# Weight splits in halves on VectorE, gate values and queries scaled on ScalarE, modulation tiles across four column groups

## The chip, the cores and the metric

One core of one Trainium2 chip runs the whole program: two layers of a transformer that denoises 512 latent tokens beside 256 context tokens. The metric is device time in microseconds, from launch to end; lower is better. Engines: PE is TensorE (matmuls), DVE VectorE, ACT ScalarE, POOL GpSimd, SP the queue that issues most DMAs.

## The reference

```python
for l in range(2):
    mod_l = silu(c) @ ada_w[l] + ada_b[l]        # shifts, scales and gates of latents
    mod_c = silu(c_ctx) @ ada_w[l] + ada_b[l]    # and of context
    hl, hc = modulate(xl, ...), modulate(xc, ...)
    yl, yc = even_mixer(...) if l == 0 else odd_mixer(...)
    xl = xl + g1 * yl
    xl = xl + g2 * conv_ffn(modulate(xl, ...))   # the same for xc in layer 0

def even_mixer(...):
    p = h @ w_in                                 # for hl and hc
    y1 = hgrn2_mixer(...)                        # gated linear attention, 4 heads, 2 directions
    u, v = gelu(p_u), rms_norm(gelu(p_v)) * vnorm_w
    y2 = u * (ws @ v + bs)                       # spatial gate, 4 groups of 128 columns
    return concat(y1, y2) @ w_out

def odd_mixer(...):
    y1 = fourier_mix(...)
    q, k, v = mla_project(...)                   # low-rank, rms_norm per head, 64 rotary columns
    return concat(y1, attend(q, k, v)) @ w_out
```

All of it is float32 with a tight tolerance.

## The kernel before, in words

**Precision.** A float32 matmul is made of three (`mm3`, L508 to L510): each operand is split into a rounded part (h, `wh`) and a remainder (l, `wl`), and h·h, h·l and l·h are summed. So each chunk of weights, 128x1024 mostly, is loaded (`raw`, SP's queue, L329), copied and rounded by ScalarE (L486), and its remainder is a subtraction: on GpSimd in one piece for the kinds in `on_pool` (L498), in two GpSimd halves for `by_half` (L495), in one half on GpSimd and one on VectorE for `down1` (L490), and on VectorE in one piece for the rest.

**Order of chunks.** `_Stream` holds the chunks in a fixed order: 4 `ev_v`, 16 `ev_in` (four a head), 8 `ev_vp`, 4 more `ev_in` (20 to 23, one a gate group), 16 `ev_out` (two passes of eight), then the feed-forward network, and layer 1. `next()` hands out one chunk and prepares the following one, at most one ahead for most kinds.

**Order of instructions.** The prologue (up to about 70 us) has its order on PE, ACT and DVE written out by hand. All else goes through a planner that orders each engine's queue by its own costs and the order of the program; `tc.high_priority(200)` lets an instruction ahead. Side work lies in generators: `tick()`, called between matmul groups, moves the generator "gla" (linear attention of one head) one step, and "ada" (modulations) at every second call; `drain()` runs one to its end.

**Mixer of layer 0.** Per head, `proj` (L795) computes four projections, while `gla` (L806) works on the head before: seven levels, at each of which PE multiplies blocks (L827, or L855 at the last two) and VectorE multiplies queries (L868) and keys (L870) by decay factors, 128x768. After the levels come states and outputs (L918, L923: squares summed on ScalarE), an inverse square root of small VectorE operations (`rsqrt`, L460 to L465), the scaling L930, a `yield`, transposes (L939) and the gating L940. Then the gate values: 8 `ev_vp` chunks, gelu and square sums (L988 to L992), `rsqrt`, six GpSimd operations that scale the values (L997), and `drain("gla")`, which ends head 3. Then, for each of four groups: projection `ev_in` 20+g, gelu (L1005), the spatial matmul (L1011), L1014 and L1018 on VectorE, and the split of the product (L1020 on ScalarE, L1021 on GpSimd).

**Output projection.** Two passes of eight chunks, the first on half of the tokens, with residuals (L1028), the norm's squares (L612, L613) and, in the second pass, the modulation of the first pass's tokens (L647 to L649) on VectorE; the up-projection follows.

**Modulations.** `ada_group` computes 16 blocks of 128 values as a product of the two condition vectors (a 32-column stationary operand) with tiles of 512 KB, (k, hf): k is the block of the contraction, hf the half of the 2048 columns. PE's array is used in four groups of 32 columns, `ps[32 * q:...]`, and a matmul streams 512 columns of the tile:

```python
for j in range(2):
    q = 2 * hf + j
    T.matmul(ps[32 * q:32 * q + 32, :], sc_pad[:, k, :], t[:, j * 512:(j + 1) * 512],
             start=(k == 0), stop=(k == KD - 1))
```

Then a copy (L585), four transposes (L589) and four additions of the bias (L594) put the values feature-major into `mods`. In layer 1 the tiles go into buffers named kt, and the generator is moved one tile at a time.

**Layer 1.** `l0.close()` (L1334) frees layer 0's buffers. Then come the token projections `od_f`, `od_kv`, `od_q`. After `lx.close()` (L1429) the embedding norms `pewb` are loaded (L1433) and the rotary table (L1435); VectorE scales the keys' rotary columns into kp0 (six operations, L1464), GpSimd copies (L1466, L1471), VectorE rotates (L1364 to L1369) and scales the table by pewb (L1470). Then, per pair of heads, keys (L1611 to L1614), values (`project_v`), queries, their statistics, and `scale_queries` (one VectorE operation L1571 and two GpSimd operations L1574), transposes and scores.

Of the kernel before, what the change touches and what calls it, by code (L numbers as in the profile page):

```python
# [415 lines left out]
def backbone(ctx: ExitStack, tc, w, xt, ada, vec, cst, msk, rop, wst, bs, pew, out):  # L416
# [68 lines left out]
    def split(kind, raw, h, l):  # L485
        S.copy(h, raw)  # L486
        if kind[:5] == "down1":
            n = raw.shape[-1] // 2
            for e, c in ((G, slice(0, n)), (V, slice(n, 2 * n))):
                e.tensor_tensor(l[:, c], raw[:, c], h[:, c].bitcast(F32), op=ALU.subtract)  # L490
            return
        if kind in by_half:
            for c in range(2):
                c = slice(c * raw.shape[-1] // 2, (c + 1) * raw.shape[-1] // 2)
                G.tensor_tensor(l[:, c], raw[:, c], h[:, c].bitcast(F32), op=ALU.subtract)  # L495
            return
        e = G if kind in on_pool else V
        e.tensor_tensor(l, raw, h.bitcast(F32), op=ALU.subtract)  # L498
# [68 lines left out]
    def ada_group(l, g, rest, by=1):  # L567
        base = (l * 3 + g) * 16
        ps = bank("ad")
        for k in range(KD):  # L570
            for hf in range(2):
                i = base + 2 * k + hf
                ada_load(i + 1)
                t = ada_raw.pop(i)
                for j in range(2):
                    q = 2 * hf + j
                    T.matmul(ps[32 * q:32 * q + 32, :], sc_pad[:, k, :], t[:, j * 512:(j + 1) * 512],  # L577
                             start=(k == 0), stop=(k == KD - 1))
            if k % by < by - 1:
# [8 lines left out]
        for b in range(4):  # L588
            T.transpose(pt[:, b * P:(b + 1) * P], asb[:, b * P:(b + 1) * P], ident)  # L589
        o = mods[l][:, g * 16:(g + 1) * 16, :].rearrange("p (j b) c -> p b j c", b=4)  # L590
        i0 = pt[:].rearrange("p (b j r) -> p b j r", b=4, r=32)[:, :, :, 0:2]
        i1 = vcol("ada_b", l * 48 + g * 16, 16).rearrange("p (j b) -> p b j", b=4).unsqueeze(3)
        for b in range(4):
            V.tensor_tensor(o[:, b], i0[:, b], i1[:, b].to_broadcast([P, 4, 2]), op=ALU.add)  # L594
        yield
# [210 lines left out]
    def gla(h, QG, FF, Y):  # L806
# [34 lines left out]
        for lv in range(7):  # L841
# [25 lines left out]
            qa = pick(QQ, 0, dd)  # L867
            V.tensor_tensor(qa, qa, pick(FF[:], NT + m, [[2 * m, nb], [-(NT + m), 2], [0, m]]), op=ALU.mult)  # L868
            ka = pick(KK, 0, dd)
            V.tensor_tensor(ka, ka, pick(FF[:], m, [[2 * m, nb], [NT - m, 2], [0, m]]), op=ALU.mult)  # L870
            ta = pick(FF[:], 0, [[NT, 2], [2 * m, nb]])
# [56 lines left out]
        for s, (a0, n) in enumerate(SEGS):  # L928
# [65 lines left out]
    rsqrt(ms[:], mr[:], 24)  # L994
    for c in range(6):
        a = vp[c // 3][:, c % 3, :].rearrange("p (g d) -> p g d", g=4)
        G.tensor_tensor(a, a, mr[:, c * 4:c * 4 + 4].unsqueeze(2).to_broadcast([P, 4, P]), op=ALU.mult)  # L997
    drain("gla")
    for g in range(4):
        ps = proj(("ev_in", 20 + g), X)  # L1000
        U = xcp.tile([P, 2, NT], F32, tag="xc", name="U")
        Y[4 + g] = xslot()
# [428 lines left out]
    l1c = ctx.enter_context(tc.tile_pool(name="l1c", bufs=1, side="right"))  # L1431
    pewb = l1c.tile([P, 128], F32, name="pewb")
    nc.scalar.dma_start(pewb[:], pew.to_broadcast([P, 128]))  # L1433
    rope_t = l1c.tile([P, 512], F32, name="rope_t")
# [25 lines left out]
    kpe = kt()  # L1460
    kp0 = tp.tile([P, 6, 64], F32, tag="t2k", name="kp0")
    kp2 = lt(F32)[:].rearrange("p a b -> p (a b)")[:, 0:768].rearrange("p (c g d) -> p c g d", c=6, g=2)
    for c in range(6):
        V.scalar_tensor_tensor(kp0[:, c, :], kvr[c][:, 256:320], kr[:, 6 + c:7 + c], pewb[:, 64:128],  # L1464
                               op0=ALU.mult, op1=ALU.mult)
    G.tensor_copy(kp2[:, 0:2, 0, :], kp0[:, 0:2, :])  # L1466
    rope(kp2[:, 2:6, 0, :], kp0[:, 2:6, :])

    t8 = rope_t[:].rearrange("p (n d) -> p n d", d=64)
    V.tensor_tensor(t8, t8, pewb[:, 0:64].unsqueeze(1).to_broadcast([P, 8, 64]), op=ALU.mult)  # L1470
    G.tensor_copy(kp2[:, :, 1, :], kp2[:, :, 0, :])  # L1471

# [95 lines left out]
    def scale_queries(p, rq, rp, s24):  # L1568
        r = r28[p % 2][:, 0:16].rearrange("p (a b) -> p a b", b=4)
        pe = rp.rearrange("p (j g d) -> p j g d", j=4, g=2)  # L1570
        V.tensor_tensor(pe, pe, r[:, :, 2:4].unsqueeze(3).to_broadcast([P, 4, 2, 64]), op=ALU.mult)  # L1571
        q4 = rq.rearrange("p j (g d) -> p j g d", g=2)
        for j in (slice(0, 2), slice(2, 4)):
            G.tensor_tensor(q4[:, j], q4[:, j], r[:, j, 0:2].unsqueeze(3).to_broadcast([P, 2, 2, P]), op=ALU.mult)  # L1574

# [304 lines left out]
```

## Time and profile before

| | us |
|---|---|
| median of 3 runs (lowest, highest) | 1649.61 (1648.12, 1650.98) |
| the profiled execution | 1649.35 |
| its span | 1647.6 |
| PE busy | 1591.9 (97%) |
| VectorE busy | 1140.8 (69%) |
| ScalarE busy | 703.4 (43%) |
| GpSimd busy | 649.1 (39%) |

The span runs from the first to the last instruction that the profiler saw on the core; the execution adds 1.75 us around it. The mean granted clock of TensorE is 0.992 of full speed. Busy time of one engine overlaps that of the others; idle time in brackets behind a row is that of the row's engine just before it.

### The profile page before, as it was taken

To read this page: it belongs to the slowest core of one execution; us is meant where nothing else is said; L and a number is where in the kernel's file an instruction comes from. 1 tells how busy PE (TensorE), PEld (TensorE's weight loads), DVE (VectorE), ACT (ScalarE), POOL (GpSimd) and SP (SyncE) were. 2 spreads that over 40 slices of the span, in tenths; PEclk is the share of its full clock that TensorE was granted. 3 is DMA by queue.
4 is the path that set the end of the run, shared out by engine and by line. 5 is a ranking of instruction groups with operands and counts; after the bars stand their busy time and mean duration, and the time that the engine had idled before them with its cause. 6 is when DMAs were issued, how large, how long until landed. Compare 5 with 4: busy or idle time off the path is not lost.

```text
span 1647.6 us, 28314 instructions
## 1 busy us (share of the span) xinstructions
PE 1591.9 (97%) x11206; PEld 1420.5 (86%) x11206; DVE 1140.8 (69%) x2134; ACT 703.4 (43%) x1328; POOL 649.1 (39%) x421
## 2 busy tenths in 40 slices
PE   8999999989999999999999999898899899999998
PEld 7777777678989999999999989676799898999997
DVE  5447675753565666676666775767874799999984
ACT  4323333523444333233332444465665555555551
POOL 1221223344625566565665513331208322323321
PEclk9999999999999999999999999999999999999999
DMA  9453434333412121222212322752105223223222
GB/s 355 159 187 116 142 116 137 120 102 103 130 50 64 61 80 55 74 77 62 80 55 75 90 68 82 250 171 93 52 27 167 90 85 108 103 90 116 103 78 77
DMA packets 53205, 175.11 MB, mean 106 GB/s; under 512 B 5712, under 2 KB 7760, under 8 KB 53072
## 3 DMA queue, kind: packets, MB, share of 16 engines
q1 hardware_dynamic: 51632, 170.66, 31.1%
q10 hardware_dynamic: 1440, 2.64, 0.4%
q8 instruction: 88, 1.44, 0.3%
q14 instruction: 45, 0.37, 0.1%
HBM read 171.18 MB, written 2.10 MB: 105 GB/s over the span
## 4 chain that ended last, share of the span: by engine, by line
PE 79%; DVE 14%; ACT 2%; DMA 2%; issue 2%; POOL 1%; DVEq 0%; SPq 0%; ACTq 0%; POOLq 0%
PE mm L508 17%; PE mm L510 16%; PE mm L509 16%; PE aux L508 7%; PE aux L509 7%; PE aux L510 7%; PE aux L577 2%; DVE qk L870 1%; DVE qk L868 1%; DVE wp L387 1%; PE aux L1143 1%; PE mm L1730 1%; DMA x<-in_xt_dram 1%; DMA raw<-in_w_dram 1%; PE aux L1749 1%
## 5 line engine op out<-in xcount | busy, mean ns | idle before, releaser
L498 POOL TENSOR_TENSOR wl<-raw,wh 128x1024 fp32r<-128x1024 f32 (+5 forms) x100 | 210.2, 2104 | 356.6 <-ACT wh L486 304.5
L486 ACT CAST wh<-raw 128x1024 fp32r<-128x1024 f32 (+5 forms) x155 | 146.5, 947 | 141.0 <-PE mm L509 63.8
L387 POOL TENSOR_TENSOR wp<-sum,wp 128x512 fp32r<-128x512 f32 x80 | 115.9, 1454 | 163.4 <-ACT wp L385 153.9
L508 PE MATMUL mm<-xt,wh 128*128 128x256 f32 (+1 forms) x384 | 135.1, 353 | 0.9 <-ACT xt L648 0.9
L510 PE MATMUL mm<-xt,wl 128*128 128x512 f32 (+1 forms) x384 | 129.4, 338 | 0.0
L509 PE MATMUL mm<-xt,wh 128*128 128x512 f32 (+1 forms) x384 | 129.3, 337 | 0.0
L509 PE MATMUL mm<-slot,wh 128*128 128x512 f32 (+1 forms) x336 | 113.4, 338 | 1.0 <-POOL slot L1253 0.7
L508 PE MATMUL mm<-slot,wh 128*128 128x512 f32 (+1 forms) x336 | 113.5, 339 | 1.0 <-ACT slot L1252 1.0
L510 PE MATMUL mm<-slot,wl 128*128 128x512 f32 (+1 forms) x336 | 113.1, 337 | 0.0
L385 ACT CAST wp<-sum 128x512 fp32r<-128x512 f32 x100 | 60.8, 620 | 122.2 <-PE aux L509 61.5
L1028 DVE SCALAR_TENSOR_TENSOR xl<-mm,mods,xl 128x512 f32<-128x512 f32 (+1 forms) x84 | 58.5, 696 | 70.7 <-PE mm L510 70.2
L495 POOL TENSOR_TENSOR wl<-raw,wh 128x512 fp32r<-128x512 f32 (+2 forms) x50 | 55.7, 1135 | 129.1 <-ACT wh L486 123.6
L387 POOL TENSOR_TENSOR wp<-raw,wp 128x512 fp32r<-128x512 f32 x60 | 80.0, 1341 | 52.3 <-ACT wp L385 52.3
L385 ACT CAST wp<-raw 128x512 fp32r<-128x512 f32 x100 | 62.1, 621 | 78.5 <-DMA raw<-in_w_dram 27.7
L508 PEld LDWEIGHTS mm<-xt,wh 128*128 128x128 f32 x384 | 72.0, 188 | 27.0 <-issue 16.8
L508 PE MATMUL mm<-kt,wp 128*128 128x256 f32 x320 | 90.4, 282 | 3.8 <-ACT t L1216 3.8
L490 POOL TENSOR_TENSOR wl<-raw,wh 128x512 fp32r<-128x512 f32 x22 | 35.7, 1622 | 138.0 <-DVE t L1245 92.3
L510 PE MATMUL mm<-kt,wp 128*128 128x256 f32 x320 | 89.8, 281 | 0.0
L509 PE MATMUL mm<-kt,wp 128*128 128x256 f32 x320 | 89.7, 280 | 0.0
L510 PEld LDWEIGHTS mm<-xt,wl 128*128 128x128 f32 x384 | 72.3, 188 | 8.2
L509 PEld LDWEIGHTS mm<-xt,wh 128*128 128x128 f32 x384 | 72.2, 188 | 8.3
L509 PE MATMUL mm<-lt,wh 128*128 128x256 f32 (+2 forms) x236 | 78.1, 331 | 1.2 <-DVE lt L1253 1.2
(390 smaller groups left out, 5272.7 us busy)
## 6 DMA issues: line engine op xcount, KB each, us to landing
raw<-in_w_dram SPq DMA_DIRECT2D x162, 512.0 KB, 3.5
ada_t<-in_ada_dram SPq DMA_DIRECT2D x80, 512.0 KB, 4.4
raw<-in_w_dram SPq DMA_DIRECT2D x31, 384.0 KB, 3.1
wp<-in_w_dram SPq DMA_DIRECT2D x20, 512.0 KB, 4.4
kt<-in_ada_dram SPq DMA_DIRECT2D x16, 512.0 KB, 7.0
raw<-in_w_dram SPq DMA_DIRECT2D x10, 256.0 KB, 2.6
xl<-in_xt_dram SPq DMA_DIRECT2D x2, 1024.0 KB, 8.0
out_dram<-xl SPq DMA_DIRECT2D x8, 256.0 KB, 2.0
```

The source lines that it names most:

```text
L385: S.copy(h, a)
L387: e.tensor_tensor(l, a, h.bitcast(F32), op=ALU.subtract)
L486: S.copy(h, raw)
L490: e.tensor_tensor(l[:, c], raw[:, c], h[:, c].bitcast(F32), op=ALU.subtract)
L495: G.tensor_tensor(l[:, c], raw[:, c], h[:, c].bitcast(F32), op=ALU.subtract)
L498: e.tensor_tensor(l, raw, h.bitcast(F32), op=ALU.subtract)
L508: T.matmul(ps, a[0], b[0], start=first, stop=False, **kw)
L509: T.matmul(ps, a[0], b[1], start=False, stop=False, **kw)
L510: T.matmul(ps, a[1], b[0], start=False, stop=last, **kw)
L577: T.matmul(ps[32 * q:32 * q + 32, :], sc_pad[:, k, :], t[:, j * 512:(j + 1) * 512], start=(k == 0), stop=(k == KD - 1))
L868: V.tensor_tensor(qa, qa, pick(FF[:], NT + m, [[2 * m, nb], [-(NT + m), 2], [0, m]]), op=ALU.mult)
L1028: V.scalar_tensor_tensor(xs, ps, gate, xs, op0=ALU.mult, op1=ALU.add)
```

## The change

Six edits:

1. `split`: the 48 chunks whose kind begins with `ev_` have their remainder computed in two halves, both on VectorE.
2. `ada_group`: each tile feeds all four column groups with 256 of its columns each, into the half hf of the accumulator; the mapping into `mods` follows.
3. `gla`: L868 and L870 get a raised priority.
4. Gate values: the six GpSimd operations become 24 ScalarE operations of 128x128, six in front of each group's projection; `gla` of head 3 is run to its last `yield` (now "tail") ahead of the groups, and what follows it runs in the ticks of the first group's projection, with `drain("gla")` behind that.
5. `pewb` has a buffer of its own, and its load is issued right after `l0.close()`; the work on the keys' rotary columns is a function, called after the first pair's values.
6. `scale_queries`: two GpSimd operations become eight ScalarE operations of 128x128 per pair.

```diff
     def split(kind, raw, h, l):
         S.copy(h, raw)
-        if kind[:5] == "down1":
+        if kind[:5] == "down1" or kind[:3] == "ev_" and kind in on_pool:
             n = raw.shape[-1] // 2
-            for e, c in ((G, slice(0, n)), (V, slice(n, 2 * n))):
+            for e, c in ((G if kind[:2] == "do" else V, slice(0, n)), (V, slice(n, 2 * n))):
                 e.tensor_tensor(l[:, c], raw[:, c], h[:, c].bitcast(F32), op=ALU.subtract)
...
-                for j in range(2):
-                    q = 2 * hf + j
-                    T.matmul(ps[32 * q:32 * q + 32, :], sc_pad[:, k, :], t[:, j * 512:(j + 1) * 512],
-                             start=(k == 0), stop=(k == KD - 1))
+                for q in range(4):
+                    T.matmul(ps[32 * q:32 * q + 32, hf * 256:(hf + 1) * 256], sc_pad[:, k, :],
+                             t[:, q * 256:(q + 1) * 256], start=k + hf == 0, stop=k + hf == KD, skip_group_check=True)
...
-            V.tensor_tensor(qa, qa, pick(FF[:], NT + m, [[2 * m, nb], [-(NT + m), 2], [0, m]]), op=ALU.mult)
+            with tc.high_priority(200):
+                V.tensor_tensor(qa, qa, pick(FF[:], NT + m, [[2 * m, nb], [-(NT + m), 2], [0, m]]), op=ALU.mult)
...
-        yield
+        yield "tail"
         Y[h] = xslot()
...
-    for c in range(6):
-        a = vp[c // 3][:, c % 3, :].rearrange("p (g d) -> p g d", g=4)
-        G.tensor_tensor(a, a, mr[:, c * 4:c * 4 + 4].unsqueeze(2).to_broadcast([P, 4, P]), op=ALU.mult)
-    drain("gla")
+    while next(bg["gla"][0]) != "tail":
+        pass
     for g in range(4):
+        for c in range(6):
+            a = vp[c // 3][:, c % 3, g * P:(g + 1) * P]
+            S.activation(a, a, AF.Copy, scale=mr[:, c * 4 + g:c * 4 + g + 1])
         ps = proj(("ev_in", 20 + g), X)
+        drain("gla")
...
     l0.close()
     lp = ctx.enter_context(tc.tile_pool(name="l1", bufs=17))
+    pewb = sm.tile([P, 128], F32, tag="pew", name="pewb", bufs=1)
+    nc.scalar.dma_start(pewb[:], pew.to_broadcast([P, 128]))
...
-    pewb = l1c.tile([P, 128], F32, name="pewb")
-    nc.scalar.dma_start(pewb[:], pew.to_broadcast([P, 128]))
...
-    kp0 = tp.tile([P, 6, 64], F32, tag="t2k", name="kp0")
...
+    def rotate_keys():
+        kp0 = tp.tile([P, 6, 64], F32, tag="t2k", name="kp0")
...
-        for j in (slice(0, 2), slice(2, 4)):
-            G.tensor_tensor(q4[:, j], q4[:, j], r[:, j, 0:2].unsqueeze(3).to_broadcast([P, 2, 2, P]), op=ALU.mult)
+        for j in range(4):
+            for g in range(2):
+                q = rq[:, j, g * P:(g + 1) * P]
+                S.activation(q, q, AF.Copy, scale=r[:, j, g:g + 1])
...
     project_v(0)
+    rotate_keys()
```

## Rows read from the trace of the kernel before

**Rows 1.** The page of the profile: busy time of each engine with its share of the span and its instructions, and the chain that ended last, by engine.

```profile
PE 1591.9 (97%) x11206; PEld 1420.5 (86%) x11206; DVE 1140.8 (69%) x2134; ACT 703.4 (43%) x1328; POOL 649.1 (39%) x421
...
PE 79%; DVE 14%; ACT 2%; DMA 2%; issue 2%; POOL 1%; DVEq 0%; SPq 0%; ACTq 0%; POOLq 0%
```

**Rows 2.** Busy time by stretch of the span (from:to in us, length, then busy us and instructions of PE, its weight load, DVE, ACT and POOL, the granted clock of PE, the DMA share and GB/s). First heads 0, 1 and 2 of the mixer, head 3 with the gate values, the gate loop, the output projection's second pass, and a part of layer 1; then two short stretches at a low clock.

```profile
115.00:172.00 57.00, 55.45 (x618) 44.56 (x617) 40.59 (x74) 20.46 (x45) 13.30 (x7) 1.00 0.40 132
172.00:230.00 58.00, 56.20 (x637) 44.88 (x639) 40.11 (x71) 20.44 (x45) 13.52 (x7) 1.00 0.39 131
230.00:287.00 57.00, 54.76 (x611) 43.82 (x600) 39.37 (x75) 20.70 (x44) 14.34 (x8) 1.00 0.38 125
287.00:346.00 59.00, 50.84 (x502) 39.39 (x501) 46.57 (x71) 25.86 (x49) 24.63 (x14) 0.99 0.44 144
346.00:426.30 80.30, 79.98 (x414) 68.00 (x413) 27.83 (x36) 22.98 (x37) 36.39 (x21) 0.99 0.28 81
426.30:455.20 28.90, 28.90 (x232) 28.15 (x230) 20.46 (x45) 17.59 (x26) 21.67 (x9) 1.00 0.52 158
...
1080.00:1190.00 110.00, 98.19 (x638) 78.75 (x636) 90.87 (x274) 67.03 (x169) 26.94 (x26) 0.98 0.30 104
...
344.20:347.70 3.50, 2.78 (x12) 2.68 (x13) 2.48 (x8) 0.84 (x2) 0.14 (x1) 0.51 0.00 2
1044.00:1047.50 3.50, 3.46 (x16) 2.83 (x20) 3.50 (x8) 2.62 (x7) 2.00 (x3) 0.51 0.02 6
```

**Rows 3.** Operations of the split by line: engine, operation, count, then duration in ns as min/median/max, first and last start in us, shapes. The third is VectorE's half of the down1 chunks.

```profile
L498 POOL TENSOR_TENSOR wl<-raw,wh x100: 731/2374/2942, 16.5 to 1298.4; 128x1024 fp32r<-128x1024 f32 x56, 128x768 fp32r<-128x768 f32 x28, 128x512 fp32r<-128x512 f32 x4, 128x640 fp32r<-128x640 f32 x4
L498 DVE TENSOR_TENSOR wl<-raw,wh x8: 1215/1225/2035, 932.4 to 970.6; 128x1024 fp32r<-128x1024 f32 x8
...
L490 DVE TENSOR_TENSOR wl<-raw,wh x22: 672/693/1606, 1327.7 to 1627.8; 128x512 fp32r<-128x512 f32 x22
```

**Rows 4.** The timeline, in four places of the heads (start and duration in us, engine, line, operation, and in brackets the idle time of the engine before it and what ended it): the four waits of PE before blocks of L827, and around the last of them a GpSimd subtraction and the VectorE product beside it; the product at 240.51 has no GpSimd operation beside it.

```profile
127.97 0.60 PE L827 MATMUL aux<-qk,scr 128*32 128x32 f32 x47 [1.52 <-DVE qk L868]
...
183.94 0.24 PE L827 MATMUL aux<-qk,scr 128*32 128x32 f32 x5 [1.61 <-DVE qk L868]
...
240.51 0.94 DVE L870 TENSOR_TENSOR qk<-qk,slot 128x768 f32<-128x768 f32 x1
...
242.45 0.63 PE L827 MATMUL aux<-qk,scr 128*32 128x32 f32 x48 [2.22 <-ACT scr L835]
...
297.76 2.39 POOL L498 TENSOR_TENSOR wl<-raw,wh 128x1024 fp32r<-128x1024 f32 x1 [2.77 <-PE aux L827]
298.00 2.97 DVE L870 TENSOR_TENSOR qk<-qk,slot 128x768 f32<-128x768 f32 x1
...
302.25 0.62 PE L827 MATMUL aux<-qk,scr 128*32 128x32 f32 x48 [1.55 <-DVE qk L868]
```

**Rows 5.** The timeline in the prologue: a wait of PE for an input tile.

```profile
65.20 0.51 PE L510 MATMUL mm<-wh,xt 128*128 128x512 f32 x1 [0.65 <-DVE xt L733]
```

**Rows 6.** The timeline near the end of the output projection's second pass: the last two modulations.

```profile
453.58 1.59 DVE L649 SCALAR_TENSOR_TENSOR xt<-aux,mods,xt 128x512 fp32r<-128x512 f32 x2
```

**Rows 7.** The timeline around the gate values: the six GpSimd operations, two of the inverse-root operations of head 3 beside and after them, and PE's next work.

```profile
337.10 6.03 POOL L997 TENSOR_TENSOR vp<-vp,mr 128x512 f32<-128x512 f32 x6 [2.50 <-DVE mr L465]
337.21 0.95 DVE L460 TENSOR_SCALAR rr<-ss 128x6 int32<-128x6 int32 x1
...
343.18 0.17 DVE L464 SCALAR_TENSOR_TENSOR rst<-rst,rr 128x6 f32<-128x6 f32 x1
...
344.92 1.54 PE L939 MATMUL aux<-ct,scr 128*128 128x128 f32 x6 [4.96 <-DVE scr L930]
```

**Rows 8.** Operations by line, as in Rows 3: a ScalarE operation of 128x128, and the GpSimd operations that scale the queries.

```profile
L923 ACT ACTIVATE junk<-aux x24: 268/277/303, 155.8 to 336.6; 128x128 f32<-128x128 f32 x24
...
L1574 POOL TENSOR_TENSOR lt<-lt,r x6: 1037/1265/1550, 1068.8 to 1168.0; 128x512 f32<-128x512 f32 x6
```

**Rows 9.** The timeline around the key embedding row (pewb): the issue of its load, the first product that needs it, and PE's wait; then, of the modulation tiles requested from 1030 to 1050, the time from request to landing.

```profile
1033.57 0.36 ACTq L1433 DMA_DIRECT2D pewb<-in_pew_dram  x1
...
1039.76 0.28 DVE L1464 SCALAR_TENSOR_TENSOR kp<-lt,rsd,pewb 128x64 f32<-128x64 f32 x1 [4.22 <-DMA pewb<-in_pew_dram]
...
1044.04 0.58 PE L508 MATMUL mm<-wh,lt 128*128 128x256 f32 x1 [3.70 <-ACT sq L1613]
...
DMA to landing us min/median/max: 3.9/7.4/10.4
```

**Rows 10.** PE's timeline around modulation matmuls, each with the instruction that follows (xN counts records, two of them to a matmul): the first tiles of the prologue with 128 columns each (L709), a pair of tiles (L577), and a lone tile, the first of nine; the last of the nine.

```profile
46.73 1.08 PE L709 MATMUL aux<-ada_t,sc_pad 128*32 128x128 f32 x32
47.73 0.50 PE L508 MATMUL aux<-wh,xt 128*128 128x512 f32 x1
...
70.18 1.06 PE L577 MATMUL aux<-ada_t,sc_pad 128*32 128x512 f32 x8
71.17 0.50 PE L508 MATMUL mm<-xt,wh 128*128 128x512 f32 x1
...
1052.96 1.05 PE L577 MATMUL aux<-kt,sc_pad 128*32 128x512 f32 x4
1053.94 0.44 PE L510 MATMUL mm<-wh,lt 128*128 128x384 f32 x1
...
1131.48 1.05 PE L577 MATMUL aux<-ada_t,sc_pad 128*32 128x512 f32 x4 [0.80 <-DMA ada_t<-in_ada_dram]
```

More of the change, by code (lines that the diff above doesn't have):

```diff
@@ L589, in ada_group @@
             T.transpose(pt[:, b * P:(b + 1) * P], asb[:, b * P:(b + 1) * P], ident)
-        o = mods[l][:, g * 16:(g + 1) * 16, :].rearrange("p (j b) c -> p b j c", b=4)
+        o = mods[l][:, g * 16:(g + 1) * 16, :].rearrange("p (f j e) c -> p f e j c", f=2, e=2)
         i0 = pt[:].rearrange("p (b j r) -> p b j r", b=4, r=32)[:, :, :, 0:2]
-        i1 = vcol("ada_b", l * 48 + g * 16, 16).rearrange("p (j b) -> p b j", b=4).unsqueeze(3)
+        i1 = vcol("ada_b", l * 48 + g * 16, 16).rearrange("p (f j e) -> p f e j", f=2, e=2).unsqueeze(4)
         for b in range(4):
-            V.tensor_tensor(o[:, b], i0[:, b], i1[:, b].to_broadcast([P, 4, 2]), op=ALU.add)
+            f, e = divmod(b, 2)
+            V.tensor_tensor(o[:, f, e], i0[:, b], i1[:, f, e].to_broadcast([P, 4, 2]), op=ALU.add)
         yield
@@ L867, in gla @@
             qa = pick(QQ, 0, dd)
-            V.tensor_tensor(qa, qa, pick(FF[:], NT + m, [[2 * m, nb], [-(NT + m), 2], [0, m]]), op=ALU.mult)
+            with tc.high_priority(200):
+                V.tensor_tensor(qa, qa, pick(FF[:], NT + m, [[2 * m, nb], [-(NT + m), 2], [0, m]]), op=ALU.mult)
             ka = pick(KK, 0, dd)
-            V.tensor_tensor(ka, ka, pick(FF[:], m, [[2 * m, nb], [NT - m, 2], [0, m]]), op=ALU.mult)
+            with tc.high_priority(200):
+                V.tensor_tensor(ka, ka, pick(FF[:], m, [[2 * m, nb], [NT - m, 2], [0, m]]), op=ALU.mult)
             ta = pick(FF[:], 0, [[NT, 2], [2 * m, nb]])
@@ L1460, in backbone @@
     kpe = kt()
-    kp0 = tp.tile([P, 6, 64], F32, tag="t2k", name="kp0")
     kp2 = lt(F32)[:].rearrange("p a b -> p (a b)")[:, 0:768].rearrange("p (c g d) -> p c g d", c=6, g=2)
[L1463 to L1471, printed above, removed]
+    def rotate_keys():
+        kp0 = tp.tile([P, 6, 64], F32, tag="t2k", name="kp0")
+        for c in range(6):
+            V.scalar_tensor_tensor(kp0[:, c, :], kvr[c][:, 256:320], kr[:, 6 + c:7 + c], pewb[:, 64:128],
+                                   op0=ALU.mult, op1=ALU.mult)
+        G.tensor_copy(kp2[:, 0:2, 0, :], kp0[:, 0:2, :])
+        rope(kp2[:, 2:6, 0, :], kp0[:, 2:6, :])
+        t8 = rope_t[:].rearrange("p (n d) -> p n d", d=64)
+        V.tensor_tensor(t8, t8, pewb[:, 0:64].unsqueeze(1).to_broadcast([P, 8, 64]), op=ALU.mult)
+        G.tensor_copy(kp2[:, :, 1, :], kp2[:, :, 0, :])
     A = []
@@ L1571, in scale_queries @@
         V.tensor_tensor(pe, pe, r[:, :, 2:4].unsqueeze(3).to_broadcast([P, 4, 2, 64]), op=ALU.mult)
-        q4 = rq.rearrange("p j (g d) -> p j g d", g=2)
-        for j in (slice(0, 2), slice(2, 4)):
-            G.tensor_tensor(q4[:, j], q4[:, j], r[:, j, 0:2].unsqueeze(3).to_broadcast([P, 2, 2, P]), op=ALU.mult)
+        for j in range(4):
+            for g in range(2):
+                q = rq[:, j, g * P:(g + 1) * P]
+                S.activation(q, q, AF.Copy, scale=r[:, j, g:g + 1])
     def turn_queries(p, rq, rp, s24):
```

## The prediction, made before the kernel was run

> **What bounds the kernel now.** I read the page's busy line and its chain of waits first. TensorE is busy for 1591.9 of 1647.6 us, so at most 55.7 us can be gained without taking work off it; the chain gives it 79% and VectorE 14%, GpSimd 1% [rows 1]. So a GpSimd time has no worth as such: what counts is where TensorE stood idle. The view by stretches [rows 2] puts that idle time: 1.55, 1.80 and 2.24 us in the first three heads of the mixer (115 to 287), 8.16 us in the fourth with the gate values (287 to 346), and none in the output projection's second pass (426.3 to 455.2).
>
> **Splits to VectorE.** 48 chunks (4 ev_v, 20 ev_in, 8 ev_vp, 16 ev_out) lose one GpSimd subtraction of 128x1024 (median 2.374 us, over 100 of several sizes) and gain two of 128x512 on VectorE. That very form is in the trace in the down1 chunks: median 0.693, minimum 0.672, maximum 1.606 us beside a GpSimd operation; a whole 128x1024 on VectorE took 1.225 [rows 3]. So 2 x 0.69 = 1.39 a chunk, 48 x 1.39 = 66 us more for VectorE and some 114 less for GpSimd. VectorE has room in a head: 40.6, 40.1 and 39.4 busy of 57 or 58 us [rows 2], to which some five splits add 7.
>
> What it removes: while a GpSimd subtraction runs, a VectorE one is held up. The 128x768 product took 2.97 us beside a subtraction that began 0.24 earlier, and 0.94 without one; TensorE then waited 1.55 for its L827 blocks [rows 4]. The four such waits are 1.52, 1.61, 2.22 and 1.55 us, nearly all of the idle time of heads 0 to 2 (1.52 + 1.61 + 2.22 = 5.35 of 5.59). The product is now also let ahead of the halves, so it can be behind one half (0.69) where it was held 2.0. I take 5.0 for heads 0 to 2 (bounds 2.5: half of the stalls come back as waits for a half; 5.6: all idle time goes). In head 3, 8.16 less the 4.96 of the next part leaves 3.2; more splits fall there (ev_vp) and VectorE is busy 46.6 of 59, so 2.6 (bounds 1.2 and 3.2). In the prologue one wait of 0.65 us on an xt tile stands beside GpSimd splits [rows 5]; VectorE's hand-written order takes the halves in its gaps: 0.6 (0 to 0.7).
>
> What it costs: in the output projection's second pass VectorE is busy 20.46 of 28.9 us [rows 2]. Seven splits x 1.39 = 9.7 make 30.2: over-full by 1.3. The last modulation there (two L649, 0.75 each) ends at 455.17 [rows 6], and the first up-projection matmuls need it within about a microsecond. I take a loss of 1.5 (bounds: 0, if residuals and statistics slide; 5, if each of the seven halves' pairs delays one evacuation by 0.7).
>
> **Gate values and the tail.** Six GpSimd operations (6.03 us in all) run from 337.10. Beside them the small inverse-root operations of the last head take 0.95 each instead of 0.17, for as long as the six run, and TensorE stands for 4.96 us until L930 has been written [rows 7]. Then the granted clock is 0.51 over 3.5 us [rows 2], the lower level, after TensorE stood: 3.5 x 0.49 = 1.7. The change takes both causes: the scaling goes to ScalarE as 24 operations of 128x128, and the matmuls that need L930 come in the ticks of the next projection. An operation of that size on ScalarE has a median of 0.277 [rows 8]: 24 x 0.28 = 6.7 us over the gate groups, on an engine busy 23 of 80 us there [rows 2]; the projection of each group hides them, and without that cover the first group's six cost 1.7. What is late next is the projection itself, if its split's halves stand on VectorE behind the root's eleven operations: 11 x 0.17 = 1.9. So 6.0 of 6.7 (bounds 4.0, 6.7). The later GpSimd operations of the gate loop stay: 0, within 0.5 either way.
>
> **Key embedding row.** At 1033.57 ScalarE's queue issues the load of pewb; VectorE stands 4.22 us until it has landed, and the keys' squares on ScalarE and TensorE behind them stand 3.70 (to 1044.04) [rows 9], with the granted clock at 0.51 over the 3.5 us after [rows 2]: 3.70 + 1.7 = 5.4. Issued right after layer 0's pools close, and with the rotation after the values' projection, that wait goes. Late next: the modulation tiles requested at 1033.56, which took up to 10.4 us to land, and TensorE gets to them earlier. I take 4.0 (bounds 1.0: only the clock's part or the wait's rest is gained; 5.4). The moved DMA costs ScalarE's queue 0.36 us, beside idle time. The rotation's six VectorE products, two GpSimd copies and the scaling of the table keep their price and move behind the values' splits.
>
> **Modulation tiles.** A 512 KB tile fed two of the four column groups with 512 columns; now it feeds all four with 256. A lone tile took 1052.96 to 1053.94, 0.98 us, and a pair that feeds four groups 70.18 to 71.17, 0.99: two groups cost as much as four. So a lone tile should take about half plus a fixed part: 0.6 (between 0.50 and 0.98). Nine lone tiles (1052.96 first, 1131.48 last) save 0.38 each, 3.4; pairs save nothing. I take 3.2, since some wait for their tile's landing as the last did (0.80) [rows 10]. Bounds 0 and 9 x 0.48 = 4.3. The added instructions (160 matmuls) cost nothing by the row of L709: 32 short records took 1.00 where eight long ones took 0.99, for as many columns [rows 10].
>
> Against this speaks a rule of the Trainium skill (TensorEngine Tiling (Array Packing), section Instruction Overhead): each matmul has some 60 cycles of overhead on TRN2, and the tiling factor should not be taken from a dimension that is already small. As an estimate from that page, 160 x 60 cycles at 2.4 GHz is 4.0 us, and the sum would be 16 instead of 20; the row of L709 disagrees.
>
> **Queries on ScalarE.** Per pair two GpSimd operations (median 1.265) become eight of 0.28 = 2.2 on ScalarE, which has 67 of 110 us busy there [rows 2, 8]. The price is about the same, and VectorE is no longer held up. 0 (bounds: a loss of 3.0, three pairs by 1.0 later; a gain of 1.5).
>
> **Sum.** 0.6 + 5.0 + 2.6 + 6.0 - 1.5 + 4.0 + 3.2 = 19.9. From the profiled execution's 1649.35 us (0.26 below the median of the runs) that is 1629.45; by the median 1629.7. I forecast 1629.5. All lower bounds together give 1649, all upper ones 1621.
>
> **Rivals.**
> A second: VectorE takes over. It gets 66 us, and as one queue in order it makes TensorE wait for half of what it waited for GpSimd. For: 46.6 of 59 busy in head 3. Against: the held-up time disappears there. Heads give 3.8 instead of 7.6, the tail 3.0, the output projection loses 5: 19.9 - 3.8 - 3.0 - 3.5 = 9.6, or 1639.8.
> A third: layer 1 gives nothing, because the tiles' landings and ScalarE's queue are late next. For: 10.4 us to landing; against: half of the tiles land in under 7.4 [rows 9]. 19.9 - 7.2 = 12.7, or 1636.7.
> A fourth, slower: the halves stand behind the products that are let ahead, and each of the 28 ev_in and ev_vp chunks begins late by one half, 0.69: 19.4 us, with the 7.6 of the heads not gained: 1649.35 + 19.4 - 12.3 = 1656.5. It decides from 12.3 / 28 = 0.44 us a chunk. For: splits are prepared only one chunk ahead. Against: a head has some five chunks in 57 us, 11 us each, and VectorE is idle for 17 of the 57.
> A fifth: the four groups don't overlap in a lone tile, and the 3.2 are gone: 1632.7; the rule on the overhead per matmul gives nearly the same time.
> That the change doesn't do what it says would show as GpSimd rows of 128x1024 before 460 us; the diff leaves no way for it.
>
> **How the numbers follow.** Forecast 0.60; the second 0.15, the third 0.12, the fourth 0.08, the fifth 0.05. The likeliest's own range is 1622 to 1636. With the second and third inside, the range is 1620 to 1641; left out are the fourth and the edges. About 0.2% (3.3 us) can be told from no change: faster takes all of the first, third and fifth and most of the second, 0.87; same 0.05; slower 0.08.
>
> **What would show it.** In the changed profile: two halves of 0.67 to 0.70 per chunk on VectorE; L868 and L870 with means near 1.0 us in the heads; TensorE's idle time below 1 us in each; no clock of 0.51 near 344 or 1044; no wait for pewb; lone modulation tiles at 0.6; the second pass of the output projection at 29 to 31 us. Wrong it is if TensorE's waits name the split in the heads, or if the second pass costs more than 5.

## The result, and the profile after

The changed kernel took 1636.01 us (median of 4 runs, 1634.70 to 1636.64) and the kernel before 1650.30 (4 runs): a ratio of 0.9911, 95% interval 0.9892 to 0.9929. The forecast was 1629.5 within 1620 to 1641. The time lies in the range and is faster, but 14 us were gained where the sum said 20. The profiled execution has a span of 1634.9 us, 12.7 less than before.

The page of the changed kernel, the same lines as [rows 1]:

```profile
PE 1588.1 (97%) x11526; PEld 1433.3 (88%) x11526; DVE 1154.3 (71%) x2230; ACT 717.1 (44%) x1376; POOL 520.8 (32%) x361
...
PE 82%; DVE 12%; ACT 3%; issue 2%; DMA 1%; POOL 0%; SPq 0%; ACTq 0%; DVEq 0%; POOLq 0%
```

GpSimd lost 128 us and VectorE gained 13.5, not 66: most of what the halves add came off other operations of VectorE that now take less (the two products of the heads 75.9 us in all before, 59.5 after). Where the 12.7 us come from is seen when the same operation is looked up in both traces (us; the first row from the span's start, each further row from the event of the row above; gains are differences of the lengths):

| from → to | before | after | gained | forecast |
|---|---|---|---|---|
| start → first matmul of a projection (L508) | 25.31 | 26.88 | -1.6 | |
| → first operation of head 0's linear attention (L813) | 75.64 | 75.33 | 0.3 | 0.6 |
| → last gelu but one of the gate values | 228.07 | 216.97 | 11.1 | 7.6 |
| → first residual of the output projection | 58.99 | 52.53 | 6.5 | 6.0 |
| → ninth residual (second pass) | 41.35 | 41.34 | 0.0 | 0 |
| → sixteenth residual (end of second pass) | 21.52 | 26.67 | -5.2 | -1.5 |
| → first scaled rounding of layer 1's latents (L1347, L1353 after) | 573.48 | 571.14 | 2.3 | |
| → 133rd rounding of a weight chunk (L486), in layer 1 as the up-projection begins | 272.89 | 274.16 | -1.3 | 7.2 |
| → last residual | 346.46 | 345.98 | 0.5 | |

(Of the 2.3, 1.7 are a stretch of 3.4 us in the kernel before, from 948.4, at a granted clock of 0.51, which the changed kernel passes at 1.00; against that stands its own low clock up to 442.2, some 1.2.)

So two stages fell out: the second pass, and layer 1's attention, which was to give 7.2 and lost 1.3. The view by stretches of the changed kernel, columns as in [rows 2]: heads 0 to 2, head 3 with the gate values, the second pass, and 6.8 us in it.

```profile
102.20:155.30 53.10, 53.10 (x641) 45.27 (x640) 34.83 (x67) 19.34 (x41) 2.49 (x1) 1.00 0.43 149
155.30:211.60 56.30, 56.03 (x670) 46.00 (x669) 38.71 (x79) 20.10 (x45) 3.81 (x3) 1.00 0.40 143
211.60:265.60 54.00, 53.80 (x642) 45.43 (x641) 39.09 (x85) 20.59 (x46) 3.79 (x3) 1.00 0.37 127
265.60:319.20 53.60, 53.46 (x590) 40.95 (x589) 39.38 (x73) 25.68 (x41) 3.80 (x3) 1.00 0.40 142
...
413.00:439.70 26.70, 23.85 (x185) 23.31 (x185) 23.95 (x46) 13.33 (x20) 5.13 (x2) 0.92 0.37 112
435.40:442.20 6.80, 6.18 (x23) 5.30 (x23) 6.25 (x10) 2.63 (x5) 1.23 (x2) 0.50 0.58 204
```

In the four heads TensorE idles for 0.00, 0.27, 0.20 and 0.14 us, where [rows 2] had 1.55, 1.80 and 2.24 in heads 0 to 2. VectorE is busy no longer than before, with the splits on it. Between the two events of the table, the first operation of the linear attention and the last gelu but one, the same view gives, before and after:

```profile
100.95:329.02 228.07, 219.28 (x2392) 173.07 (x2389) 157.43 (x259) 85.01 (x168) 64.48 (x31) 1.00 0.40 133
102.21:319.18 216.97, 216.36 (x2538) 177.62 (x2537) 151.98 (x300) 85.69 (x167) 13.89 (x10) 1.00 0.40 140
```

So 8.2 of the 11.1 us gained are idle time of TensorE (8.79 to 0.61), and 2.9 are busy time. VectorE's operations in the four heads, by line (count, busy us, mean ns):

```profile
L872 DVE TENSOR_TENSOR qk<-qk,slot 128x768 f32<-128x768 f32 x28 | 29.8, 1064 | 9.5 <-ACT scr L835 8.2
L869 DVE TENSOR_TENSOR qk<-qk,slot 128x768 f32<-128x768 f32 x28 | 29.7, 1062 | 2.8 <-PE aux L855 2.3 <-PE aux L827 0.4
L490 DVE TENSOR_TENSOR wl<-raw,wh 128x512 fp32r<-128x512 f32 x41 | 27.7, 690 | 10.0 <-ACT wh L486 10.0
```

The two products (L868 and L870 before, one of them 2.97 us long beside GpSimd in [rows 4]) have means of 1.06, and a half takes 0.69, as [rows 3] said. The tail, for [rows 7], in the timeline:

```profile
330.82 0.87 PE L941 MATMUL aux<-ct,scr 128*128 128x128 f32 x6 [0.35 <-DVE scr L932]
```

4.96 us of waiting have become 0.35.

**The second pass.** The timeline of the changed kernel:

```profile
431.43 2.36 POOL L498 TENSOR_TENSOR wl<-raw,wh 128x1024 fp32r<-128x1024 f32 x1 [60.62 <-DVE acc L613]
431.99 2.35 DVE L490 TENSOR_TENSOR wl<-raw,wh 128x512 fp32r<-128x512 f32 x1
...
431.43 5.15 POOL L498 TENSOR_TENSOR wl<-raw,wh 128x1024 fp32r<-128x1024 f32 x2 [60.62 <-DVE acc L613]
431.99 5.13 DVE L490 TENSOR_TENSOR wl<-raw,wh 128x512 fp32r<-128x512 f32 x2
...
434.40 0.39 PE L510 MATMUL mm<-slot,wl 128*128 128x256 f32 x1 [2.20 <-DVE wl L490]
437.18 0.58 PE L510 MATMUL mm<-slot,wl 128*128 128x256 f32 x1 [0.62 <-DVE wl L490]
```

GpSimd has done nothing for 60 us and starts on the first two chunks of the up-projection, whose splits stayed with it. Beside them the two halves of an output chunk take 5.13 us instead of 1.39: the first ends 0.55 after GpSimd's operation has ended (434.34 and 433.79). TensorE waits 2.20 us, gets the lower clock from 435.4 to 442.2 (the row 435.40:442.20), and waits another 0.62 in it. Up to the fourteenth residual the pass had lost only 0.3 to 0.5 us.

**ScalarE's queue in layer 1.** The timeline of ScalarE, and TensorE's next wait:

```profile
1093.12 0.58 ACT L1618 COPY lt<-mm 128x512 f32<-128x512 f32 x1
1096.37 2.45 ACT L1581 ACTIVATE lt<-lt,r 128x128 f32<-128x128 f32 x8 [2.67 <-DVE r L465]
1098.72 0.57 ACT L1620 ACTIVATE sq<-mm 128x512 f32<-128x512 f32 x1
...
1099.80 0.39 PE L508 MATMUL mm<-kt,lt 128*128 128x256 f32 x1 [2.75 <-ACT pr L1746]
```

The eight scalings of a pair of queries wait for the inverse root on VectorE, 2.67 us, and run for 2.45. Behind them stands the square of the keys' last part (L1620), whose copy (L1618) was done at 1093.7, and behind that the softmax's exponentials (L1746), for which TensorE waits.

**The early row.** The wait for pewb is gone, and TensorE is 5.5 us further ahead in the queries' transposes than at the start of the stage. Then this stands in the timeline:

```profile
1034.82 1.16 POOL L1629 TENSOR_TENSOR lt<-lt,r 128x512 f32<-128x512 f32 x1
1035.00 2.12 DVE L1629 TENSOR_TENSOR lt<-lt,r 128x512 f32<-128x512 f32 x2
...
1038.05 2.05 DVE L1354 SCALAR_TENSOR_TENSOR lt<-aux,vt,lt 128x512 fp32r<-128x512 f32 x3
...
1038.84 0.44 PE L510 MATMUL mm<-wh,lt 128*128 128x384 f32 x1 [3.24 <-DVE lt L1354]
```

The keys' scaling (beside its GpSimd third) and the end of the rotation come first on VectorE, and TensorE waits 3.24 us for the remainder of the query latents (L1354). Then the low clock is there again, in the view by stretches:

```profile
1039.50:1042.90 3.40, 3.40 (x16) 2.15 (x15) 0.64 (x2) 0.00 (x0) 0.00 (x0) 0.51 0.16 57
```

### The profile page after: what moved, and what is told of

The parts are those of the page before. It is cut to its first block, busy times and chain, and to the rows that moved or that the text cites. A ratio compares the mean times of both kernels' runs of the same rounds, so it can differ in the third digit from the quotient of the medians.

```text
span 1634.9 us, 29027 instructions
## 1 busy us (share of the span) xinstructions
PE 1588.1 (97%) x11526; PEld 1433.3 (88%) x11526; DVE 1154.3 (71%) x2230; ACT 717.1 (44%) x1376; POOL 520.8 (32%) x361
## 4 chain that ended last, share of the span: by engine, by line
PE 82%; DVE 12%; ACT 3%; issue 2%; DMA 1%; POOL 0%; SPq 0%; ACTq 0%; DVEq 0%; POOLq 0%
PE mm L508 18%; PE mm L510 17%; PE mm L509 17%; PE aux L508 7%; PE aux L509 7%; PE aux L510 7%; PE aux L576 2%; DVE wp L387 1%; PE aux L1147 1%; DVE wl L490 1%; PE mm L1738 1%; PE aux L827 1%; PE aux L855 1%; PE aux L1757 1%; PE aux L897 1%
## 5 line engine op out<-in xcount | busy, mean ns | idle before, releaser
L486 ACT CAST wh<-raw 128x1024 fp32r<-128x1024 f32 (+5 forms) x155 | 146.6, 947 | 143.8 <-PE mm L509 72.6
L498 POOL TENSOR_TENSOR wl<-raw,wh 128x768 fp32r<-128x768 f32 (+6 forms) x52 | 94.6, 1820 | 177.8 <-ACT wh L486 89.7
L508 PE MATMUL mm<-xt,wh 128*128 128x256 f32 (+1 forms) x384 | 135.5, 354 | 0.1
L510 PE MATMUL mm<-xt,wl 128*128 128x512 f32 (+1 forms) x384 | 129.2, 337 | 0.0
L510 PE MATMUL mm<-slot,wl 128*128 128x512 f32 (+1 forms) x336 | 113.3, 338 | 2.8 <-DVE wl L490 2.8
L508 PE MATMUL mm<-slot,wh 128*128 128x512 f32 (+1 forms) x336 | 113.5, 339 | 1.0 <-ACT slot L1256 1.0
L490 DVE TENSOR_TENSOR wl<-raw,wh 128x512 fp32r<-128x512 f32 x118 | 88.8, 773 | 26.6 <-ACT wh L486 19.5
L508 PE MATMUL mm<-kt,wp 128*128 128x256 f32 x320 | 90.3, 282 | 3.8 <-ACT t L1220 3.8
L510 PE MATMUL mm<-kt,wp 128*128 128x256 f32 x320 | 89.8, 280 | 0.0
L508 PEld LDWEIGHTS mm<-xt,wh 128*128 128x128 f32 x384 | 72.3, 189 | 18.0 <-issue 8.2
L510 PEld LDWEIGHTS mm<-xt,wl 128*128 128x128 f32 x384 | 72.4, 189 | 8.3
L490 POOL TENSOR_TENSOR wl<-raw,wh 128x512 fp32r<-128x512 f32 x22 | 35.7, 1622 | 137.7 <-DVE t L1249 92.2
```

The lines of the kernel that those rows point to most:

```text
L508: T.matmul(ps, a[0], b[0], start=first, stop=False, **kw)
L510: T.matmul(ps, a[1], b[0], start=False, stop=last, **kw)
```

## The experiments

Twelve kernels, each timed beside the kernel before on the same chip. All but the last two are the changed kernel with one edit. Ratios are to the kernel before; the changed kernel stands at 0.9911 (0.9892 to 0.9929).

| run | edit to the changed kernel | us | ratio, 95% interval |
|---|---|---|---|
| e1 | first two up-projection splits also on VectorE | 1632.55 | 0.9888 (0.9869 to 0.9907) |
| e2 | output projection's splits back on GpSimd | 1633.01 | 0.9884 (0.9863 to 0.9906) |
| e3 | rotation behind turn_q | 1634.28 | 0.9900 (0.9885 to 0.9916) |
| e4 | modulation tiles as before | 1640.04 | 0.9933 (0.9909 to 0.9957) |
| e5 | queries scaled on GpSimd | 1629.50 | 0.9868 (0.9852 to 0.9884) |
| e6 | pewb and rotation as before | 1632.43 | 0.9891 (0.9876 to 0.9906) |
| e7 | keys' scaling and rotation behind turn_q | 1635.37 | 0.9908 (0.9893 to 0.9923) |
| e8 | splits of ev_v, ev_in, ev_vp on GpSimd | 1640.74 | 0.9943 (0.9926 to 0.9960) |
| e9 | no raised priority | 1637.82 | 0.9917 (0.9899 to 0.9934) |
| e10 | queries' scaling on ScalarE, issued later | 1629.59 | 0.9865 (0.9851 to 0.9880) |
| e11 | e2 and e5 together | 1625.44 | 0.9842 (0.9827 to 0.9857) |
| e12 | e2, e5 and e6 together | 1624.12 | 0.9838 (0.9818 to 0.9859) |

**The second pass (e1, e2).** Held up, or over-full?

```diff
-        if kind[:5] == "down1" or kind[:3] == "ev_" and kind in on_pool:
+        n_up0[0] += kind == "up0"
+        if kind[:5] == "down1" or kind[:3] == "ev_" or kind == "up0" and n_up0[0] <= 2:      # e1
+        if kind[:5] == "down1" or kind[:3] == "ev_" and kind != "ev_out":                    # e2
```

> The changed kernel, but the first two splits of the up-projection, which GpSimd ran at 431.43 for 5.15 us in the changed kernel, are halves on VectorE too. Theory one (held up): the two halves of the last output chunk took 5.13 us instead of 1.39 because GpSimd ran beside them; without a GpSimd operation they take 0.69 each, TensorE's waits of 2.20 and 0.62 there fall below 0.5 in sum and the low clock after them (435.4 to 442.2) goes: 1636.0 - 4.5 = 1631.5, ratio to the kernel before 0.9885. Theory two (over-full): VectorE has too much work in the second pass; four more halves (2.8 us) make the waits longer: 1636 to 1639, ratio 0.991 to 0.993.

> The changed kernel with the 16 output-projection splits back on GpSimd in one piece, and the other 32 on VectorE. Both theories of the second pass expect its length back at that of before (residual 8 to residual 15 in 21.5 us instead of 26.7), so 1636.0 - 5.2 = 1630.8, ratio 0.988. If the 5.2 had another cause (the up-projection's first chunks, the loads), the pass stays long: 1636, ratio 0.991.

The timeline of e1 at the place (L493 is its L490, L513 its L510):

```profile
431.75 1.29 DVE L493 TENSOR_TENSOR wl<-raw,wh 128x512 fp32r<-128x512 f32 x2
...
432.49 0.39 PE L513 MATMUL mm<-slot,wl 128*128 128x256 f32 x1 [0.54 <-DVE wl L493]
```

With four more halves on VectorE the two halves take 1.29 us, the wait is 0.54, no low clock follows (1.00 over the pass), and the pass is 23.4 us long, where the nine kernels that leave it as it is have 26.0 to 26.7 (before: 21.5). So the hold-up cost 2.6 to 3.3 us. In e2, with neither the hold-up nor the halves, the pass lasts 21.5, as before: the 1.9 us that e1 keeps go with the halves on VectorE, but TensorE idles for only 0.6 of them, and how an over-full queue makes up the rest is not shown. The low clock adds little within the pass: e9 passes it at 1.00 and still needs 26.0 us, with longer waits:

```profile
414.09:440.13 26.04, 22.66 (x187) 22.18 (x187) 23.87 (x46) 12.81 (x20) 5.12 (x2) 1.00 0.36 111
```

Both runs came out some 3 us faster than the changed kernel by the medians (1631.5 and 1630.8 expected, 1632.55 and 1633.01 measured), but the intervals overlap with its own: the times alone do not show the gain, the lengths of the pass do.

**The queries (e5, e10).**

```diff
         V.tensor_tensor(pe, pe, r[:, :, 2:4]...)                  # scale_queries
-        for j in range(4):
-            for g in range(2): ... S.activation(q, q, AF.Copy, scale=r[:, j, g:g + 1])
+        for j in (slice(0, 2), slice(2, 4)): G.tensor_tensor(q4[:, j], ...)   # e5; e10: the loop above, in turn_queries
```

> The changed kernel with the scaling of the queries back on GpSimd (two operations a pair). Theory one: the eight ScalarE operations a pair put ScalarE's queue behind, and the waits for ScalarE at 1063.25 (2.38, asb) and 1096.78 (2.75, pr) shrink without them: 1636.0 - 2.5 = 1633.5, ratio 0.9897. Theory two (the same price on either engine, as forecast): within 1 us of the changed kernel, ratio 0.9905 to 0.9918. Theory three: GpSimd's operations hold VectorE up again: 1637 to 1639, ratio 0.9925.

> The changed kernel with the eight ScalarE operations a pair kept, but issued at the head of turn_queries, behind the pair's keys. Theory one: their price is what stood behind them on ScalarE while they waited for the inverse root (2.67 us at 1096.37, then 2.45 of work, with the keys' squares and PSUM evacuations behind): issued later, most of the 6.5 us that the GpSimd version won comes back: 1636.0 - 5 = 1631, ratio 0.988. Theory two: it is ScalarE's added work itself (24 operations) or their later result: within 1.5 us of the changed kernel, ratio 0.990 to 0.992.

Both give 6.5 us by the medians, clear of the changed kernel's interval; e5 more than its best theory. Its attention stage is 8.2 us shorter than before where the changed kernel's is 1.3 longer. e10 does the same 24 operations on ScalarE, only with the keys ahead of them, so neither the work nor the time at which the scaled queries come is the price. Its timeline of ScalarE, at the same place:

```profile
1094.14 0.58 ACT L1618 COPY lt<-mm 128x512 f32<-128x512 f32 x1
1094.62 0.60 ACT L1620 ACTIVATE sq<-mm 128x512 f32<-128x512 f32 x1
1097.38 0.99 ACT L1583 ACTIVATE lt<-lt,r 128x128 f32<-128x128 f32 x3 [2.17 <-DVE r L465]
```

The square follows its copy at once, and the scaling waits for the root with nothing in need behind it. Part of the gain is clock. The view by stretches of the whole attention stage, for the changed kernel, e5, e10, and e11 (below), whose code in this stage is that of e5:

```profile
1010.85:1285.02 274.17, 250.65 (x1893) 220.57 (x1892) 193.60 (x572) 153.44 (x372) 79.03 (x69) 0.96 0.34 121
1010.30:1274.98 264.68, 245.25 (x1893) 216.61 (x1892) 193.08 (x572) 147.56 (x347) 86.51 (x75) 0.98 0.35 125
1011.93:1277.47 265.54, 245.95 (x1893) 216.82 (x1892) 193.86 (x572) 153.83 (x371) 79.81 (x69) 0.98 0.36 125
1005.66:1274.46 268.80, 249.60 (x1893) 220.21 (x1892) 192.70 (x572) 147.45 (x347) 86.55 (x75) 0.96 0.35 123
```

TensorE idles (length less busy time) for 23.5 us in the changed kernel, 19.4 and 19.6 in e5 and e10, and 19.2 in e11. So 4 us of waiting went in all three; its waits for the exponentials fell from 4.3 us to 3.3 in e5 and 1.9 in e10, and the rest is spread over other waits. In e5 and e10 the granted clock also rose from 0.96 to 0.98, and their stages are 9.5 and 8.6 us shorter than the changed kernel's; in e11 it stayed at 0.96, and the stage is 5.4 shorter. Why the clock differs between e5 and e11 is not shown.

**The early row (e3, e6, e7).**

```diff
     scale_keys(0, *k0)            # e7: moved behind the loop too
     project_v(0)
-    rotate_keys()
     fill(2)
     for k in range(3):
         turn_q(k)
+    rotate_keys()                 # e3, e7; e6: pewb's load and the rotation where they were
```

> The changed kernel with the call of rotate_keys moved behind the loop of turn_q. Theory one: the 5.5 us that the early pewb gave are lost again because the rotation's operations (1029 to 1038.1 on VectorE and GpSimd) stand ahead of the remainder of turn_q (L1354), for which TensorE waited 3.24 us at 1038.84, and the low clock after it cost 1.7; behind the loop these go: 1636.0 - 4.5 = 1631.5, ratio 0.9885. Theory two: something is late next whatever the order (modulation tiles, queries that need the scaled table): within 1 us of the changed kernel, ratio 0.9905 to 0.9915.

> The changed kernel with the load of pewb and the rotation of the keys where they were before. Theory one: the early load won 5.5 us by 1049 and the next wait (3.24 us before L1354's remainder, and the low clock behind it) took nearly all of it: with the old place the one wait comes back and the other goes, within 1.5 us of the changed kernel, ratio 0.990 to 0.9925. Theory two (the forecast's: it is worth 4.0): 1640, ratio 0.9938.

> The changed kernel with the scaling of the first pair's keys (two operations of 2.12 us in all on VectorE, one on GpSimd beside them) and the rotation both issued behind the loop of turn_q. Theory one: what delays L1354 is the queue ahead of it on VectorE, of which moving the rotation alone left the key scaling in place; with both behind it the wait of 3.24 falls below 1 and part of the low clock goes: 1636.0 - 3.5 = 1632.5, ratio 0.989. Theory two: the planner's order or the next wait (keys' transposes, queries) takes it again: within 1.5 us of the changed kernel, ratio 0.990 to 0.992.

e3 and e7 missed: TensorE still waited 3.46 and 3.56 us before the same matmul. The timeline of e7 there:

```profile
1036.18 2.14 DVE L1629 TENSOR_TENSOR lt<-lt,r 128x512 f32<-128x512 f32 x2
1038.24 2.06 DVE L1354 SCALAR_TENSOR_TENSOR lt<-aux,vt,lt 128x512 fp32r<-128x512 f32 x3
1039.04 0.69 PE L510 MATMUL mm<-wh,lt 128*128 128x384 f32 x1 [3.56 <-DVE lt L1354]
1040.22 0.41 DVE L1370 TENSOR_TENSOR lt<-kp,rope_t 128x256 f32<-128x256 f32 x1
```

In both traces the rotation itself (from L1370 on) now stands behind L1354, so the rotation alone does not make the wait. The six products with pewb and the keys' scaling (L1629) still stand ahead of it, in e7 too, which moved that call: the planner orders VectorE's queue by its own priorities. Counted from the stage's start the wait ends 1.2 to 1.3 us earlier than in the changed kernel, but TensorE arrives 1.5 earlier. Whether a queue without the keys' scaling would end the wait stays open. In e6, with the old place, the attention stage is 0.1 us longer than that of before, in the changed kernel 1.3; but the changed kernel's code for this stage also stands in e1, e2, e8 and e9, where the stage takes 272.1 to 274.4 us, so a difference of 1.1 can't be told from none. The forecast 4 us are not there: the wait that part 5 removes and the one that it lets in about cancel. e6 ended 3.6 us faster by the medians (the intervals overlap); in the profiles 3.4 us lie at the start (below).

**The modulation tiles (e4).**

```diff
-                for q in range(4):
-                    T.matmul(ps[32 * q:32 * q + 32, hf * 256:(hf + 1) * 256], ..., t[:, q * 256:(q + 1) * 256], ...)
+                for j in range(2): ... 512 columns for two groups, and the mapping of before
```

> The changed kernel with the modulation tiles feeding two column groups as before. Theory one (the groups work side by side, lone tiles halve): the 3.9 us less of modulation matmuls in the heads (2 of them a wait) and 2.6 in layer 1 come back in part: 1636.0 + 3.5 = 1639.5, ratio 0.993. Theory two (the saving is hidden by other waits): within 1 us, ratio 0.991. Theory three (a price for each added matmul): faster, 1632 to 1635.

Theory one: 4.0 us lost by the medians (the intervals overlap). In the profiles 5.0 are lost: 3.6 in layer 1's attention, 1.5 in the stage before it, whose length moves as much between other runs, and none in the heads, whose 11.0 us of gain are there without it. The stage of e4:

```profile
1012.27:1290.01 277.74, 256.33 (x1765) 216.67 (x1764) 193.23 (x572) 153.39 (x372) 78.82 (x69) 0.96 0.35 119
```

At the same granted clock as in the changed kernel it is 3.6 us longer, outside the 272.1 to 274.4 of the five kernels with the changed kernel's code there, with 5.7 us more of busy time on TensorE and 2.1 less of idle time. A pair and a lone tile in PE's timeline of the changed kernel, for the rows of [rows 10]:

```profile
70.84 1.07 PE L576 MATMUL aux<-ada_t,sc_pad 128*32 128x256 f32 x16
71.84 0.50 PE L508 MATMUL mm<-xt,wh 128*128 128x512 f32 x1
...
1043.22 0.64 PE L576 MATMUL aux<-kt,sc_pad 128*32 128x256 f32 x8
1043.79 0.45 PE L508 MATMUL mm<-wh,lt 128*128 128x384 f32 x1
```

The lone tile takes 0.57 us, where it took 0.98 and 0.6 was forecast; the pair takes 1.00 with twice the matmuls, where it took 0.99.

**The heads (e8, e9).**

```diff
+        if kind[:5] == "down1" or kind == "ev_out":               # e8
-            with tc.high_priority(200):                           # e9: both
```

> The changed kernel with the 32 splits of ev_v, ev_in and ev_vp back on GpSimd in one piece; the output projection's stay on VectorE and L868 and L870 keep their priority. Theory one (held up by GpSimd): from the first head to the first gate value 11.0 us were won, and they go: 1636.0 + 9 = 1645, ratio 0.997. Theory two (the priority alone won them): within 2 us of the changed kernel, ratio 0.991 to 0.9925.

> The changed kernel without the raised priority of L868 and L870. From the first head to the last gate-value chunk the changed kernel won 11.1 us, and with the splits back on GpSimd 5.1 were left. Theory one: those 5 are the priority's, so without it the heads lose 3 to 5: 1636.0 + 4 = 1640, ratio 0.9935. Theory two (the priority does nothing once the splits are halves on VectorE): within 1 us in the heads, ratio 0.991.

From the first head to the last gelu, 11.1 us were gained; e8 has 5.1 of them and e9 9.1. So the halves are worth 6.0 with the priority there, and the priority 2.0 with the halves there. The 3.1 left come with either of the two alone, or from something else: no run is without both. e8 was expected to lose 9 and lost 4.7; e9's 2 are in the stage, and its median is not clear of the changed kernel's.

**Both together (e11, e12).**

> The changed kernel with the queries' scaling back on GpSimd and the output projection's splits back on GpSimd. The two lie in different stages, so the theory expects the sum of the two runs alone: 1636.0 - 6.5 - 4.5 = 1625, ratio 0.984. If one gain only moved a wait that the other also removes: 1628 to 1630, ratio 0.986 to 0.988.

> The same with the load of pewb and the rotation where they were before. Theory one (part 5 gives nothing or loses 1.1 us, as the stage showed): 1624 to 1625, ratio 0.9835. Theory two: without the scaling on ScalarE in the way, the early pewb is worth its 4: 1629, ratio 0.9865.

The two gains add: 1625.44, 25.6 us faster than before and clear of the changed kernel's interval. In their profiles the second pass is 21.5 us long, as before, and layer 1's attention 4.1 and 4.4 us shorter than before, where e5 had 8.2 at the higher clock: the stage of a single profile moves by some us. Without part 5 the time is 1624.12; the intervals overlap almost wholly, so neither a gain nor a loss by part 5 is seen there.

## Why the prediction was right, and where its sum was wrong

Right in time, range and sign, and in part by luck. In the profile 8.5 us of the forecast are missing in layer 1's attention and 3.7 in the second pass; 3.5 more came in the heads than was taken, and 2.3 in a stage for which nothing was forecast. Without those two the time would have been some 1642, just outside the range. Two of the prediction's own signs came out against it: the second pass cost more than 5, with TensorE's waits naming the split in it, and a granted clock of 0.51 stands in layer 1 again. By its steps:

- **Splits, heads**: right in mechanism. Durations of halves and products, and the end of the waits, came as read. The term was mis-sized: 7.6 against 11.1. It counted the idle time that the rows of before show, and of that 8.2 went; the other 2.9 are busy time of TensorE, which the sum took as fixed. Why the matmuls took less is not shown.
- **Tail and gate values**: right, 6.0 against 6.5.
- **Second pass**: -1.5 taken, -5.2 measured, just past the bound of 5. The step that failed is "over-full by 1.3": it used the hold-up only as a thing that goes. 16 chunks went to VectorE while the up-projection's splits behind them stayed on GpSimd, so the hold-up came back at the seam (2.6 to 3.3 us by e1). The Trainium skill (SBUF — State Buffer, sections SBUF: two separate sides and Who interferes with whom) calls the port pair that VectorE shares with GpSimd an exclusive lock, held for a whole instruction. The rows agree: a half that began 0.56 us after a GpSimd operation ended 0.55 after its end.
- **Modulation tiles**: right, 3.2 against 3.6 in the profile. The Trainium skill's rule on some 60 cycles for each matmul (TensorEngine Tiling (Array Packing), section Instruction Overhead) would have left nothing, by the prediction's estimate of 4.0 us. The pair disagrees for this case: sixteen records take 1.00 us where eight took 0.99.
- **Queries on ScalarE**: 0 taken with a bound of -3; measured -6.5 (e5), some 4 of it waits of TensorE, the rest in its busy time, where the clock comes in. This is the step that cost most. It compared the price of the operations and did not ask what the added wait would stand in front of: the square that could have started at 1093.7 started at 1098.72. The wait (2.67 us) and the work (2.45) are seen in the rows. e10 has the time and the idle time of e5 with all 24 operations still on ScalarE, so the price was their place in the queue.
- **Key embedding row**: 4.0 taken; the 5.4 of the wait and its clock did come, and were lost 8 us later to a queue on VectorE that the prediction had not followed (its "late next" named the modulation tiles). The load, gone out early, cost some 1.1 us more at the start (below).

The rival nearest to the time was the third (1636.7, layer 1 gives nothing). It had the stage and, with ScalarE's queue, half of the cause; the landings were not it: TensorE waits for them for 0.8 us in the stage, before and after.

## What to carry to other kernels

When work leaves GpSimd for VectorE, look at the seam where the next work is still on GpSimd: there the two met here, and the hold-up that was removed stood again (5.13 us for two halves instead of 1.39). An operation that is cheap on an idle engine is priced by what it waits for and what is queued behind it; issue it behind the work that is ready. A wait that is removed is worth only the distance to the next one: 5.5 us here, lost 8 us later. Where a planner orders the queue, moving a call in the source may not move the instruction.

## What had not been expected

The load of pewb was to go out after layer 0, at about 1000 us. In the changed kernel its buffer is free from the start, and it went out at 11.5 us, into the loads of the prologue. The view of DMA from 8 to 28 us: the changed kernel's rate in GB/s in 40 slices of 0.5 us, and the issue of pewb (64 KB, us to landing):

```profile
GB/s 406 424 410 408 403 426 391 406 404 414 426 418 410 404 391 189 142 107 220 431 401 418 418 426 451 377 401 401 442 410 401 410 410 418 434 410 401 401 393 410
...
pewb<-in_pew_dram ACTq DMA_DIRECT2D x1, 64.0 KB, 6.9
```

and e6's, which loads it late:

```profile
GB/s 399 406 399 432 387 418 414 404 418 401 418 418 410 393 418 418 401 401 418 442 377 401 393 393 418 418 426 393 402 410 418 410 418 402 434 377 401 401 402 410
```

For four slices (15.5 to 17.5) the rate is 107 to 220 instead of some 405: (4 x 405 - 658) x 0.5 / 405 = 1.2 us of loading lost to 64 KB, and the modulation tiles of the prologue land later. The same dip stands in all eleven kernels with the early load and in none of the three without. The first matmul of a projection began at 24.6 to 27.9 us in the eleven, and at 23.52 in both kernels without it that have the other edits. Of that, 1.1 us are shown to be the load: e3 (24.61) and e6 (23.52) both have a granted clock of 1.00 up to that matmul, and the difference is near the 1.2. The other ten passed a stretch at the low clock there, as the changed kernel did:

```profile
18.90:25.70 6.80, 6.31 (x56) 5.79 (x52) 3.21 (x14) 1.12 (x3) 0.00 (x0) 0.50 1.03 414
```

The kernel before has such a stretch without the early load and began at 25.31, so what the clock cost at the start can't be put down to the load.
